# The MLP's second product in half-height matmul pairs: 64 rows of the array for one token tile, 64 for another

## The chip, the cores and the metric

The kernel runs on one core of a Trainium2 chip, in one launch. The metric is the device time of that launch in microseconds, as the median of several runs. The core's engines are TensorE (PE in the profile; its weight loads are listed apart as PEld), VectorE (DVE), ScalarE (ACT), GpSimd (POOL) and SyncE (SP). Each has its own queue of instructions, and the queues wait for one another through semaphores.

## The reference, cut to what matters

One layer of a hybrid transformer block on 1024 tokens of width 1024: a token mixer (a pooling branch and a neighbourhood attention with context keys), a projection, and then the MLP with a squared ReLU. All in float32. The part around the change:

```python
def _sq_relu_mlp(h, w1, w2):
    return jnp.square(jax.nn.relu(h @ w1)) @ w2

    x = x + gt1 * _rmsnorm(mix_x, g_post_mix[l])
    y_x = _sq_relu_mlp(_modulate(x, g_pre_mlp[l], sh2, sc2), w_mlp_in[l], w_mlp_out[l])
    x = x + gt2 * _rmsnorm(y_x, g_post_mlp[l])
```

`h @ w1` is 1024x1024 by 1024x4096, the second product is 1024x4096 by 4096x1024.

## The kernel before, in words

Products in float32 are made of three matmuls in the type fp32r (`three`, lines 197 to 200): each operand is split into a high part and a low part that holds the remainder, and high x high, high x low and low x high are summed in PSUM. In the trace these matmuls are listed as f32, like the plain f32 matmuls of the attention.

Both MLP products are done by a Strassen-like scheme of seven half-size products in place of eight. The hidden layer (4096 wide) is kept in DRAM in seven combinations of its quarters (`hidd`: A11, A12, A22, S1 to S4), each as 8 pages of 128 x 1024: 128 hidden units as rows, two units' blocks of 512 tokens side by side. The second product reads them back. Its seven products are called P1 to P7. Each has 8 groups; a group is one page of hidden values (hi and lo) with one page of weight combinations (hi and lo).

A group (`group`) sums into four PSUM banks, one for each tile of 128 tokens (`ps[0]` to `ps[3]`; the hidden values are the stationary operand, the weights the moving one with 512 columns). For each token tile (`token_sums`) it walks the two blocks j of the page, three matmuls each: 6 matmuls a tile, 24 a group, all with the full 128 rows and 128 columns of the array. The tile's six matmuls go to its bank one after another, then the next tile follows.

The four lists of banks are x, y, v and z. P1 runs alone into x (8 groups). P6 into y and P2 into x take turns, group by group; then P7 into v and P5 into z; then P4 into v and P3 into z for four groups, and two more groups of P3. The last two groups of P3 and the last four of P4 are done at the end, token tile by token tile, with `token_sums` directly, so that the ends of the rows (`finish`, `end`) overlap with the matmuls of later tiles.

Around the groups: `prepare` (called at the start of each group) loads and splits the operands of the item three places ahead: SP issues the DMAs (`hidden`, `columns`), ScalarE makes the high part (`high_part`, line 146), VectorE the low part (`low_part`, line 152) and the weight combinations. The order on PE, ScalarE, VectorE and SP in this part is as written in the code (`in_order`); POOL is left out of that. POOL has little to do here: before the second group of P1 it issues the four DMAs of `mod_gain` (line 243), before the fourth the four DMAs of `mod_out` (line 253), which wait for a product of VectorE (line 247) and that for eight small matmuls (line 236); at the end it makes one reciprocal root per row tile (`rsqrt_of`, line 140).

Elsewhere the kernel has two kinds of matmuls that use only a part of the array: the attention's scores (line 984) contract over 64 rows, for two heads in the two row halves, into two banks; the modulation sums (lines 236 and 401) use 32 of the array's columns, four of them side by side.

Of the kernel before, what the change touches and what calls it, by code (L numbers as in the profile page):

```python
# [18 lines left out]
P = 128  # L19
# [7 lines left out]
HD = 64  # L27
# [53 lines left out]
def hybrid_block(ctx, tc, x, ctx_in, w_mod, b_mod, gp1, gp2, w_in, pool_w, rpb, w_out, w1, w2, vectors,  # L81
                 mask, edge, out):
    nc = tc.nc
# [19 lines left out]
    @contextmanager  # L103
    def in_order(*engines):
        block = nc.cur_bb
        n = len(block.bb.instructions)
        last = {}
        yield last
        assert nc.cur_bb is block
        for i in block.bb.instructions[n:]:  # L110
            if i.engine in engines:
                if i.engine in last:
                    tc.add_manual_dep(i, last[i.engine].name,
                                      mybir.DependencyInfo(mybir.DependencyClass.NoSync, mybir.DependencyReason.DATA),
                                      reason="order")
                last[i.engine] = i
# [80 lines left out]
    def three(ps, ahi, alo, bhi, blo, first, last, more=False):  # L197
        nc.tensor.matmul(ps, ahi, bhi, start=first, stop=False, skip_group_check=more)  # L198
        nc.tensor.matmul(ps, ahi, blo, start=False, stop=False, skip_group_check=more)  # L199
        nc.tensor.matmul(ps, alo, bhi, start=False, stop=last, skip_group_check=more)  # L200
# [70 lines left out]
    with tc.tile_pool(name="ps1", bufs=6, space=PSUM) as ps1, tc.tile_pool(name="tmp1", bufs=3) as tmp:  # L271

        def bank(name):
            if name[:2] == "pm" or name in ("pxt1_0", "pxt0_2", "pxt1_7", "pct2", "pct3"):
                return lasting(name)
            return ps1.tile([P, 512], F32, tag="mm", name=name)
# [7 lines left out]
        last = startup.enter_context(in_order(ET.PE, ET.Activation, ET.DVE, ET.SP, ET.Pool))  # L284
# [276 lines left out]
        for k in range(KT):  # L561
            for i in range(2):
                o = (k % 2) * 256 + i * P
# [178 lines left out]
        with tc.issue_after(last[ET.DVE]), tc.issue_after(last[ET.Activation]):  # L742
            for i in range(2):
                ps = bank(f"pvc{i}")
# [49 lines left out]
        rows = [("sc", 4, k) for k in range(4, KT)] + [("a", 2, k) for k in range(KT)]  # L794
# [35 lines left out]
        for n, m in enumerate((4, 5, 6, 7, 0, 1, 2, 3)):  # L830
            ps = bank(f"pv{m}")
# [99 lines left out]
        with in_order(ET.PE, ET.Pool, ET.Activation, ET.DVE, ET.SP) as pooling:  # L931
            banks = {of: [bank(f"p{of}{j}") for j in range(2)] for of in "KQ"}
            use(-1)
            for step, (n, of, j) in enumerate([(n, of, j) for n, of in products for j in range(2)]):
                half_product(n, of, j, banks[of])
                use(step)
                if step in (5, 9, 17):
                    name = {5: "S1", 9: "S4", 17: "S3"}[step]
# [4 lines left out]
                if step in (7, 11):  # L943
                    name = {7: "S4", 11: "S3"}[step]
# [11 lines left out]
    with (  # L956
# [195 lines left out]
        with in_order(ET.PE, ET.Activation, ET.DVE, ET.SP) as projected:  # L1152
# [7 lines left out]
            for i in range(N + 4):  # L1160
# [12 lines left out]
                if i > 3:  # L1173
                    weighed(i - 4)
                    if i % 8 == 3:
                        j = i // 8 - 1
# [22 lines left out]
                if 8 < i < N and i % 8 == 7:  # L1199
                    j = i // 8 - 1  # L1200
# [9 lines left out]
                else:  # L1210

                    t = i - N
# [51 lines left out]
    with tc.tile_pool(name="ps2", bufs=6, space=PSUM) as ps2:  # L1264
# [6 lines left out]
      with ExitStack() as tmp2:  # L1271
# [28 lines left out]
        rows, root = {}, {}  # L1300
# [233 lines left out]
        NG = NPAIR // 2  # L1534
# [256 lines left out]
        made = {}  # L1791
        coming = list(items)

        def prepare():
            i = coming.pop(0) if coming else None
            if i:
                made[i] = operands(*i, split_pages if i in (("P4", NG - 2), ("P4", NG - 1)) else None)
# [39 lines left out]
        with tc.issue_after(first[ET.PE]), in_order(ET.PE, ET.Activation, ET.DVE, ET.SP):  # L1837
# [12 lines left out]
            def token_sums(ps, t, groups, first, last, more):  # L1850
                n = 2 * len(groups)
                for j in range(n):
                    a, w = groups[j // 2]
                    o = (j % 2) * 512
                    three(ps[t], a[0][:, o + t * P : o + (t + 1) * P], a[1][:, o + t * P : o + (t + 1) * P],
                          w[0][:, o : o + 512], w[1][:, o : o + 512], first and j == 0, last and j == n - 1, more=more)

            def group(ps, name, g, more=False, last=False):
                prepare()
                for t in range(4):  # L1860
                    token_sums(ps, t, [made.pop((name, g)) if t == 3 else made[name, g]], g == 0 and not more,
                               last or g == NG - 1, more)


            sq = [sm(f"sy{h}", NT) for h in range(2)]
            rows = {}
# [33 lines left out]
            for g in range(NG):  # L1900
                if g == 1:
                    gain = mod_gain(gp2, page("gpb")[:, :256], nc.gpsimd)
                if g == 3:
                    mod_gate("b", acc_b[-1], gain, lambda name: pg)
                    mod_out("b", acc_b[-1])
                group(x, "P1", g)
# [4 lines left out]
            for g in range(NG):  # L1911
                group(y, "P6", g)
                if g == NG // 2:
                    G2 = gate_page("b")
                if g == NG - 1:
                    u2 = halves("u2")
                    for t in range(4):
                        nc.vector.tensor_tensor(u2[t], y[t], s1[t], add)
                group(x, "P2", g, more=True)
# [71 lines left out]
```

## Time and profile before

| | |
|---|---|
| time, median of 3 runs | 1032.65 us (1032.61 to 1032.82) |
| span of the profiled execution | 1030.8 us; its own time lies some 1.85 us above, if it was like the median |
| PE busy | 1017.8 us, 5782 matmuls |
| PE weight loads | 834.2 us, 5782 |
| DVE, ACT, POOL busy | 751.8, 543.7, 110.7 us |
| second product, first matmul to last | 718.0 to about 1023 us |
| granted TensorE clock | 0.998 on average |

The span runs from the first to the last instruction of the profiled execution. A matmul's duration in the trace is the time from its issue to its last result; matmuls overlap, so the price of one in a row of many is the distance between two starts, which a count over a stretch of time gives. `x16` behind a row of the order of time means that 16 instructions of a kind were merged; the row's time then runs from the first start to the last end. In a row of a group, `128*128 128x512` is the array's rows and columns in use and then the moving operand.

### The profile page before, as it was taken

The numbers are of one execution on the slowest core, as the hardware profiler recorded it, in microseconds if no ns is written. First come the engines' busy times: TensorE is split into PE (matmuls) and PEld (weight loads), VectorE is DVE, ScalarE is ACT, GpSimd is POOL, SyncE is SP. The second block draws the span as 40 slices with busy tenths as digits, with TensorE's granted clock in tenths as the row PEclk, the third lists the DMA queues.
The fourth block names the chain that finished last, engine by engine and source line by source line (L and its number), as shares of the span: only waits on it lengthen the run. The fifth ranks groups of instructions, "written<-read, shape, count | busy, mean of one in ns | idle before, by whom it ended". The sixth has DMA issues, their size and how long they took to land.

```text
span 1030.8 us, 15588 instructions
## 1 busy us (share of the span) xinstructions
PE 1017.8 (99%) x5782; PEld 834.2 (81%) x5782; DVE 751.8 (73%) x1187; ACT 543.7 (53%) x941; POOL 110.7 (11%) x168
## 2 busy tenths in 40 slices
PE   8999999999999999999999999999999999999997
PEld 6788888877887888888888888888888888888885
DVE  5588767858996587878998887855766666547576
ACT  7573255328887556776655544555543334334431
POOL 3011200244311311310000000000000000000001
PEclk9999999999999999999999999999999999999999
DMA  9999798632337866795786666637967766555556
GB/s 343 332 255 338 246 265 296 204 86 80 72 95 194 203 180 200 253 237 168 267 269 210 204 210 214 205 122 241 327 220 271 248 226 220 202 180 189 176 182 211
DMA packets 123132, 222.68 MB, mean 216 GB/s; under 512 B 9456, under 2 KB 55152, under 8 KB 123056
## 3 DMA queue, kind: packets, MB, share of 16 engines
q1 hardware_dynamic: 96560, 171.14, 50.4%
q0 software_dynamic: 9360, 19.58, 9.5%
q10 hardware_dynamic: 17136, 30.97, 8.0%
q8 instruction: 45, 0.74, 0.3%
q14 instruction: 31, 0.25, 0.1%
HBM read 168.16 MB, written 52.45 MB: 214 GB/s over the span
## 4 chain that ended last, share of the span: by engine, by line
PE 95%; DMA 2%; ACT 1%; DVE 1%; issue 0%; SPq 0%; DVEq 0%; POOLq 0%; ACTq 0%
PE pu L449 4%; PE S L984 4%; PE pa L1060 3%; PE phv L198 3%; PE phz L198 3%; PE phx L198 3%; PE pyx L198 3%; PE phx L200 3%; PE phv L199 3%; PE phx L199 3%; PE pyx L199 3%; PE pyx L200 3%; PE pyv L199 3%; PE pyv L198 3%; PE pyz L199 3%; PE pyz L198 3%
## 5 line engine op out<-in xcount | busy, mean ns | idle before, releaser
L1007 ACT ACTIVATE sp<-sp,nm 128x640 f32<-128x640 f32 (+1 forms) x64 | 51.4, 803 | 20.0 <-DVE nm L998 19.6
L1577 ACT ACTIVATE c<-c 128x512 f32<-128x512 f32 x48 | 30.3, 632 | 47.0 <-DVE c L1697 28.2
L146 ACT CAST wpS<-S 128x512 fp32r<-128x512 f32 x64 | 38.7, 616 | 26.4 <-PE phv L200 9.2
L198 PE MATMUL phx<-thB,wpA 128*128 128x512 f32 x128 | 50.2, 392 | 0.0
L200 PE MATMUL phx<-thB,wpA 128*128 128x512 f32 x128 | 49.8, 389 | 0.0
L199 PE MATMUL phx<-tlB,wpA 128*128 128x512 f32 x128 | 49.8, 389 | 0.0
L152 DVE TENSOR_TENSOR wpS<-S,wpS 128x512 fp32r<-128x512 f32 x64 | 43.4, 685 | 8.3 <-ACT wpS L146 8.3
L998 DVE CUSTOM_DVE_ANT_0 sp<-S,tab 128x640 f32<-128x640 f32 (+1 forms) x56 | 42.9, 803 | 8.8 <-PE S L984 7.3
L1578 ACT ACTIVATE c<-c 128x512 f32<-128x512 f32 x48 | 30.3, 631 | 15.1 <-DVE sa L1660 12.3
L140 POOL TENSOR_TENSOR ry<-vy,nhalf 128x1 f32<-128x1 f32 x8 | 5.9, 740 | 280.7 <-DVE vy L138 280.7
L198 PEld LDWEIGHTS phx<-thB,wpA 128*128 128x128 f32 x128 | 24.0, 188 | 5.5 <-ACT s L1628 0.5
L984 PE MATMUL S<-kT,q 64*128 64x384 f32 (+1 forms) x128 | 27.9, 495 | 0.3 <-DVE nm L998 0.3
L200 PEld LDWEIGHTS phx<-thB,wpA 128*128 128x128 f32 x128 | 24.0, 188 | 5.0
L199 PEld LDWEIGHTS phx<-tlB,wpA 128*128 128x128 f32 x128 | 24.0, 188 | 4.9
L1060 PE MATMUL pa<-pt,v 128*64 128x128 f32 x352 | 25.9, 279 | 0.6 <-ACT px L1040 0.2
L1045 DVE COPY pt<-T 128x512 f32<-128x512 f32 x32 | 22.0, 686 | 5.5 <-PE T L1026 5.5
L198 PE MATMUL phv<-thT,wpA 128*128 128x512 f32 x64 | 25.1, 392 | 0.0
L198 PE MATMUL phz<-thB,wpS 128*128 128x512 f32 x64 | 25.0, 391 | 0.0
L200 PE MATMUL phv<-thT,wpA 128*128 128x512 f32 x64 | 24.9, 389 | 0.0
L199 PE MATMUL phv<-tlT,wpA 128*128 128x512 f32 x64 | 24.9, 389 | 0.0
L200 PE MATMUL phz<-thB,wpS 128*128 128x512 f32 x64 | 24.9, 389 | 0.0
L199 PE MATMUL phz<-tlB,wpS 128*128 128x512 f32 x64 | 24.9, 389 | 0.0
(1100 smaller groups left out, 3359.7 us busy)
## 6 DMA issues: line engine op xcount, KB each, us to landing
b<-in_w SPq DMA_DIRECT2D x64, 512.0 KB, 4.2
hrS<-hdS SPq DMA_DIRECT2D x32, 512.0 KB, 5.1
hrA<-hdA SPq DMA_DIRECT2D x24, 512.0 KB, 5.5
wm<-in_w_mod SPq DMA_DIRECT2D x16, 512.0 KB, 9.7
wa_0w<-in_w SPq DMA_DIRECT2D x16, 512.0 KB, 5.3
wa_1w<-in_w SPq DMA_DIRECT2D x16, 512.0 KB, 4.5
hdA<-c ACTq DMA_DIRECT2D x32, 256.0 KB, 2.8
hdS<-sa ACTq DMA_DIRECT2D x32, 256.0 KB, 2.7
```

The costliest lines, as they stand in the source:

```text
L146: nc.scalar.copy(hi, src)
L152: nc.vector.tensor_tensor(lo, src, hi.bitcast(F32), sub)
L198: nc.tensor.matmul(ps, ahi, bhi, start=first, stop=False, skip_group_check=more)
L199: nc.tensor.matmul(ps, ahi, blo, start=False, stop=False, skip_group_check=more)
L200: nc.tensor.matmul(ps, alo, bhi, start=False, stop=last, skip_group_check=more)
L449: nc.tensor.matmul(pus[b][j], wk(wgt, k, low, j * P, P), r, start=(k == 0 and n == 0), stop=(k == KT - 1 and n == 2))
L984: nc.tensor.matmul(S[e][:, c0 : c0 + keys.shape[1]], q[hs, cols], keys[hs], start=True, stop=True)
L998: nc.vector.tensor_tensor_reduce(out=to, in0=s, in1=bt, scale=1.0, scalar=BIG, op0=add, op1=ALU.min, accum_out=nm)
L1007: nc.scalar.activation(sp, sp, AF.Exp, bias=least[i, e], scale=-1.0, accum_out=sums[i][:, e : e + 1])
L1060: nc.tensor.matmul(pa[e * HD : (e + 1) * HD, cols], v[:, f : f + HD], turns[i][:, e, c] if c < 4 else fifths[i][:, :, (e + 1) * HD : (e + ...
L1577: nc.scalar.activation(r, src, AF.Relu)
L1578: nc.scalar.activation(r, r, AF.Square)
```

## The change

`group` no longer calls `token_sums`. It goes through the group in four quarters with two token tiles each: (0, 1), (2, 3), (1, 0), (3, 2). Within a quarter every former matmul of 128 rows becomes two of 64 rows: the rows 0 to 63 of the operands for the first tile named, the rows 64 to 127 for the second, next to each other in the order of PE, into two different banks. In the third and fourth quarter the tiles change places, so that after all four each bank has had both halves of the contraction. 24 matmuls of 128 rows become 48 of 64 rows, with 512 moving columns as before.

The two halves of the array never write one bank at the same time: the first matmul of a quarter waits for the end of the last matmul of the quarter that used these two banks before. The wait goes over POOL: a `nop` on POOL's queue, after the last matmul of each quarter, and a dependency of the first matmul of the next quarter on the same banks upon that `nop`. There are four such `nop`s in a group, 200 in all. The dictionary `crossings` keeps the last one of each list of banks and pair of tiles, also across groups. The matmuls at the end (`token_sums` on z and v) stay as they were.

```diff
+            crossings = {}
+
+            def after(i, before):
+                tc.add_manual_dep(i.ins, before.ins.name,
+                                  mybir.DependencyInfo(mybir.DependencyClass.Sync, mybir.DependencyReason.DATA),
+                                  reason="rows of the array")
+
             def group(ps, name, g, more=False, last=False):
                 prepare()
-                for t in range(4):
-                    token_sums(ps, t, [made.pop((name, g)) if t == 3 else made[name, g]], g == 0 and not more,
-                               last or g == NG - 1, more)
+                a, w = made.pop((name, g))
+                begin, end = g == 0 and not more, last or g == NG - 1
+                for n, tokens in enumerate(((0, 1), (2, 3), (1, 0), (3, 2))):
+                    crossing = crossings.pop((id(ps), n % 2), None)
+                    for j in range(2):
+                        o = j * 512
+                        for i, (al, wl) in enumerate(((0, 0), (0, 1), (1, 0))):
+                            for rows, t in zip((slice(0, HD), slice(HD, P)), tokens):
+                                mm = nc.tensor.matmul(ps[t], a[al][rows, o + t * P : o + (t + 1) * P], w[wl][rows, o : o + 512],
+                                                      start=begin and n < 2 and j + i == 0,
+                                                      stop=end and n > 1 and j == 1 and i == 2, skip_group_check=True)
+                                if crossing:
+                                    after(mm, crossing)
+                                    crossing = None
+                    crossings[id(ps), n % 2] = nc.gpsimd.nop()
+                    after(crossings[id(ps), n % 2], mm)
```

## The prediction

> **What bounds the kernel now.** First the page's span, busy shares and chain, then one stretch of the second product, then its order of time.
>
> ```profile
> span 1030.8 us, 15588 instructions
> PE 1017.8 (99%) x5782; PEld 834.2 (81%) x5782; DVE 751.8 (73%) x1187; ACT 543.7 (53%) x941; POOL 110.7 (11%) x168
> ...
> PE 95%; DMA 2%; ACT 1%; DVE 1%; issue 0%; SPq 0%; DVEq 0%; POOLq 0%; ACTq 0%
> ```
> ```profile
> 736.00:1016.00 280.00, 280.00 (x1237) 231.85 (x1236) 183.34 (x178) 114.07 (x136) 6.21 (x9) 1.00 0.64 221
> ```
> ```profile
> 800.14 0.39 PE L200 MATMUL pyy<-t_3h,hhS_3l 128*128 128x512 f32 x1
> ...
> 802.86 0.39 PE L200 MATMUL pyx<-b_3h,hhA_3l 128*128 128x512 f32 x1
> ```
> ```profile
> 800.15 0.19 PEld L198 LDWEIGHTS pyx<-b_3h,hhA_3h 128*128 128x128 f32 x1
> ```
>
> TensorE is the bound: 95% of the chain, and busy for all 280.00 us of the stretch from 736 to 1016 us, at a granted clock of 1.00. The 1237 matmuls there come every 280.00/1237 = 226.4 ns (I use 226.5). VectorE is busy for 183 of the 280 us and ScalarE for 114, so nobody else is near. A matmul's 0.39 us is its latency, not its price: they overlap. The load for the next matmul starts 0.01 us after a matmul starts and takes 0.19 us, inside the 0.2265. So the loads are already beside the matmuls, and the question of this change is whether a pair of half-height matmuls goes through in less than, just as much as, or more than 226.5 ns.
>
> **The change part by part.** *The matmuls.* 50 groups of 24 go through the edited function (8 each of P1, P6, P2, P7, P5, 4 of P4, 6 of P3): 1200 full matmuls become 1200 pairs of 64 rows, 2400 instructions, each half with a load of its own. The 144 of the tail stay. No trace row has a 64-row fp32r matmul; the nearest are the attention scores, 64-row f32 pairs on two banks:
>
> ```profile
> 227.05 0.30 PEld L984 LDWEIGHTS S<-kT,q 64*128 64x128 f32 x4 [0.35 <-issue]
> 227.06 0.92 PE L984 MATMUL S<-kT,q 64*128 64x384 f32 x4
> ...
> 227.80 0.60 PE L984 MATMUL S<-kcT,q 64*128 64x256 f32 x4
> 228.24 0.14 PEld L1026 LDWEIGHTS pa<-ident,rb 64*128 64x128 f32 x1 [0.24 <-DVE rb L1013]
> 228.24 0.27 PE L1026 MATMUL pa<-ident,rb 64*128 64x64 f32 x1
> ```
> ```profile
> 66.54 1.91 PE L564 MATMUL pct<-ident,c 128*128 128x128 f32 x16
> 68.20 0.71 PE L449 MATMUL pu<-hx,wu1h 128*128 128x512 f32 x2
> ```
> ```profile
> 734.38 0.64 PE L236 MATMUL pgb<-accb,ones 128*32 128x256 f32 x8
> 734.95 0.50 PE L198 MATMUL pyx<-b_3h,hhA_3h 128*128 128x512 f32 x1
> 735.89 0.42 DVE L247 TENSOR_TENSOR accb<-pgb,gpb 128x256 f32<-128x256 f32 x1
> ```
> ```profile
> L984 PE MATMUL S<-kcT,q x128: 376/376/480, 218.8 to 319.6; 64*128 64x256 f32 x128
> ```
> (An f32 product shows as two matmuls, a transpose as one.) Two pairs of 256 columns take 228.24 - 227.80 = 0.44 us, 0.22 a pair, 0.86 ns a column. Eight of 256 columns in quarters of the array's width (L236) take 0.64 us with the latency of the last, about 0.38 for this width: 0.26 for the first four, so four side by side go at the pace of two. Full-height f32 matmuls exist only as transposes (L564), (68.20 - 66.54)/16 = 0.104 us for 128 columns, 0.81 ns a column. So halves do go through side by side, in about the time of one full matmul of the same width, and not faster than it. Carried over to fp32r: a pair costs what the full matmul costs, 226.5 ns, and 1200 pairs change the sum by 0. The added loads are covered too: four take 0.30 us, side by side, under the running pair.
>
> Could the pair shed something? By its pace an f32 matmul of 256 columns occupies the array about as long as an fp32r one of 512. Durations, beside the 376 of L984:
>
> ```profile
> L198 PE MATMUL pyx<-b_0h,hhA_0h 128*128 128x512 f32 x16 | 6.2, 389 | 0.0
> ```
> ```profile
> L690 PE MATMUL pkc<-hc,wk0h x8: 387/395/398, 76.5 to 85.3; 128*128 128x512 f32 x8
> ...
> L690 PE MATMUL pkc<-hc,wk0l x8: 277/280/281, 76.7 to 85.5; 128*128 128x256 f32 x8
> ```
> An fp32r matmul of 512 is 13 ns longer than the f32 half of 256: 389 against 376. With the same latency past the stream, 389 - 226.5 = 163, the streams are 226 and 213. If that is a price of exchanging weights in the whole array, halves may hide it: up to -13 x 1200 = -15.6 us. If it is a price of streaming 4-byte columns, they can't. The fp32r rows of 512 and 256 columns (387/395 and 277/280) differ by 110 to 115 ns; 13 ns per matmul whatever its width would leave 213/2 = 107 between them, 13 ns spread over 512 columns gives 113. Nearest is the second, so I take 0 and keep -15.6 as the lower end. The upper end for the stream is no concurrency at all, +226.5 x 1200 = +272 us.
>
> [...]
>
> *Change of array shape.* Rows where 64-row pairs follow and precede full matmuls:
>
> ```profile
> 218.51 0.39 PE L200 MATMUL pqv<-S3h,wQT3l 128*128 128x512 f32 x1
> 218.83 0.70 PE L984 MATMUL S<-kcT,q 64*128 64x256 f32 x4
> 219.36 0.60 PE L984 MATMUL S<-kT,q 64*128 64x256 f32 x4
> 219.89 0.50 PE L198 MATMUL pqv<-hx,wQT4h 128*128 128x512 f32 x1
> 220.23 0.40 PE L199 MATMUL pqv<-hx,wQT4h 128*128 128x512 f32 x1
> ```
> Into the pairs: 0.32 instead of 0.2265, and 0.53 instead of 0.44: +0.18. Out: 0.53 instead of 0.44, then 0.34 instead of 0.2265: +0.20. The new kernel goes in at P1 and out at the tail, +0.4 us; the gate's column-tiled matmuls in the middle already pay for such a change today.
>
> *The crossings.* 200 nops on POOL's queue, each behind the last matmul of a quarter group; 192 matmuls wait for one (the first two of each of the four lists of sums have none). Within a group, and between groups of one product that follow each other, six pairs of the other quarter lie between, 6 x 226.5 = 1.36 us, of which 0.39 goes until the last matmul has ended: 0.97 us of cover for PE to POOL to PE. No row shows that trip; its parts:
>
> ```profile
> 228.43 0.82 DVE L998 CUSTOM_DVE_ANT_0 sp<-S,tab 128x640 f32<-128x640 f32 x1 [0.25 <-PE S L984]
> 229.18 0.08 DVE L998 DVE_READ_ACCUMULATOR2_ANT nm<- 128x1 f32 x1
> 229.32 1.33 PE L984 MATMUL S<-kT,q 64*128 64x384 f32 x3 [0.30 <-DVE nm L998]
> ```
> ```profile
> 707.32 1.99 POOL L243 DMA_DIRECT2D gpb<-in_gp  x4 [111.49 <-PE phz L200]
> 736.59 1.93 POOL L253 DMA_DIRECT2D gb<-accb  x4 [27.28 <-DVE accb L247]
> ...
> 1019.25 0.55 POOL L140 TENSOR_TENSOR ry<-vy,nhalf 128x1 f32<-128x1 f32 x1 [2.62 <-DVE vy L138]
> ```
> From PE to a waiting engine 0.03 (228.43 after 227.80 + 0.60), to POOL up to 0.28 (736.59 after 735.89 + 0.42); the nop between 0 and POOL's 0.55 for its smallest tensor operation; back to PE 0.06 (229.32 after 229.26). Sum 0.09 to 0.89 us: inside 0.97 at both ends, so I cost the steady crossings at 0; with the cover gone each microsecond of lateness costs some 120 us (100 crossings within groups and 18 between groups have only this cover, the others a whole group of the other product).
>
> POOL's own DMAs stand in the same queue. Those of L243 are now behind the nops of P1's first group, at about 723.8 instead of 707.32, busy to 725.8; they must have landed by 734.4. The second group's first nop slips to 725.8, and is wanted at 726.2: 0 to 0.5, I take 0.1. Those of L253 end at 736.59 + 1.93 = 738.52; the nop behind them lets go a matmul that is due at 734.95 + 0.3 + 12 x 0.2265 = 737.97: +0.6 to +1.2, I take 0.7. After that POOL has nothing until the tail.
>
> *The end of each product.* Two token tiles now end with the third quarter of the last group and two with the fourth, instead of one per quarter. Their readers are four copies or sums of about 0.7 us; the sums are written again a whole group (5.4 us) later, so 0.
>
> Sum: 0 + 0.4 + 0.1 + 0.7 = +1.2 us on the span of 1030.8, 1032.0. The median of the runs, 1032.65, lies 1.85 above the profiled span; with the same 1.85 the time is 1033.9, +0.12%. That is less than the 0.2% (2.1 us) which a measurement of this kernel tells from no change.
>
> **The rivals.** *A, forecast: pairs at the old pace, crossings covered.* 1033.9; own range 1031.5 to 1037.5 (a fee of 3 ns a pair more would be +3.6).
>
> *B, the halves shed the 13 ns.* 1033.9 - 15.6 = 1018.3 in full; at the 0.22 us of the f32 pair, -6.5 x 1200 = -7.8, 1026.1. The 13 ns over the f32 row speak for it, the 256-column fp32r rows and the equal price of f32 pairs and f32 full matmuls against it.
>
> *C, the crossing takes the place of what was gained or more: the trip over POOL is longer than its cover.* It decides from 0.97 + 2.1/120 = 0.99 us on; a trip of 1.2 us costs 0.23 x 120 = 28, 1061. For it: the upper bound of the parts, 0.89, is near, and a pair that runs faster shortens the cover. Against it: the lower sum is 0.09.
>
> *D, fp32r halves don't run side by side*, because two full-rate 4-byte streams or two full-rate writes into PSUM don't fit, which f32 pairs at half the column rate never asked for: +272 us, 1306. For it: no row shows such a pair; against it only the f32 pairs. [...]
>
> **How the numbers follow.** A 0.42, B 0.28, C 0.20, D 0.10. A's range lies across +0.2%, so it gives 0.24 to no change and 0.18 to slower; B is faster; C and D are slower: 0.28, 0.24, 0.48. The predicted time is A's. The range takes in B and C, 1018 to 1062, and leaves out D and the far ends of C.
>
> **What would show it.** In the changed trace, two 64-row matmuls some 0.01 us apart on two banks and the next two 0.2265 us after: A; 0.213 to 0.22: B; 0.45: D. Waits of PE on POOL at the first matmul of the third and fourth quarter: C; one alone near 738 us is the step of L253. The gpb transfers move behind 723 us. The forecast falls if any price repeats 1200 or 120 times that the f32 rows don't have.

## The result, and the profile after

| | before | changed |
|---|---|---|
| time, median of 20 runs | 1032.73 us | 1034.77 us |
| ratio | | 1.0017, 95% interval 1.001 to 1.0023 |
| span of the profiled execution | 1030.8 us | 1033.3 us |

The change costs 0.17% by the ratio; the two medians differ by 2.0 us (0.20%). 1033.9 was predicted (+0.12%). The profiled execution of the changed kernel is the longest of its twenty runs (1035.77 us; the median of their spans is 1032.6), so single places in it can cost more than they do in a typical run. The page of the changed kernel, and a stretch of 250 us of the second product of both kernels (first the changed one), with the busy time and count of each engine:

```profile
span 1033.3 us, 18193 instructions
PE 1019.2 (99%) x6982; PEld 834.6 (81%) x6982; DVE 751.9 (73%) x1187; ACT 543.5 (53%) x941; POOL 110.9 (11%) x168
...
PE 93%; DMA 3%; ACT 1%; DVE 1%; issue 1%; SPq 0%; POOL 0%; DVEq 0%; POOLq 0%; ACTq 0%
```
```profile
741.00:991.00 250.00, 250.00 (x2210) 206.83 (x2208) 156.97 (x143) 101.49 (x116) 0.00 (x0) 1.00 0.65 217
```
```profile
741.00:991.00 250.00, 250.00 (x1105) 207.01 (x1104) 156.88 (x143) 101.52 (x117) 0.00 (x0) 1.00 0.63 217
```

1200 more matmuls and loads, and in the same 250 us exactly twice as many halves as full matmuls: 2210 against 1105. A pair takes 250/1105 = 226.2 ns, as a full matmul did. (The count takes in matmuls that lie across the ends of the stretch; from start to start it is 226.7 ns on average in both kernels.) In order of time the two halves of a pair stand merged as x2, one pair every 0.226 us:

```profile
800.04 0.39 PE L1875 MATMUL pyy<-t_3h,hhS_3l 64*128 64x512 f32 x2
800.27 0.39 PE L1875 MATMUL pyy<-t_3h,hhS_3h 64*128 64x512 f32 x2
800.50 0.39 PE L1875 MATMUL pyy<-t_3l,hhS_3h 64*128 64x512 f32 x2
```

What was lost stands in three places. At the start of P1 and at the tail, where the array changes its shape:

```profile
717.90 0.39 PE L200 MATMUL phv<-thT,wpA 128*128 128x512 f32 x1
718.22 0.50 PE L1875 MATMUL pyx<-b_0h,hhA_0h 64*128 64x512 f32 x2
718.56 0.40 PE L1875 MATMUL pyx<-b_0l,hhA_0h 64*128 64x512 f32 x2
```
```profile
992.48 0.39 PE L1875 MATMUL pyz<-b_5h,hhS_5l 64*128 64x512 f32 x2
992.80 0.50 PE L198 MATMUL pyz<-b_6h,hhS_6h 128*128 128x512 f32 x1
993.14 0.40 PE L199 MATMUL pyz<-b_6l,hhS_6h 128*128 128x512 f32 x1
```

Each time 0.32 and 0.34 instead of twice 0.2265: 0.2 us in, 0.2 us out. And near 738 us, in the group before which POOL issues the DMAs of the gate:

```profile
737.99 0.39 PE L1875 MATMUL pyx<-b_3h,hhA_3l 64*128 64x512 f32 x2
739.62 0.50 PE L1875 MATMUL pyx<-b_3h,hhA_3h 64*128 64x512 f32 x2 [1.24 <-POOLq L1881]
739.95 0.39 PE L1875 MATMUL pyx<-b_3l,hhA_3h 64*128 64x512 f32 x2
```
```profile
728.79 1.98 POOL L243 DMA_DIRECT2D gpb<-in_gp  x4 [132.68 <-PE pyx L1875]
738.29 1.93 POOL L253 DMA_DIRECT2D gb<-accb  x4 [7.53 <-DVE accb L247]
```
```profile
737.58 0.42 DVE L247 TENSOR_TENSOR accb<-pgb,gpb 128x256 f32<-128x256 f32 x1 [1.96 <-DMA gpb<-in_gp]
```

The pair due at 738.22 starts at 739.62, and the next comes 0.33 later: 1.4 + 0.1 us. It waits for a nop (L1881) that stands on POOL's queue behind three of the four DMAs of L253. These are late because the product of L247 was held for 1.96 us by the transfer of L243, and that one was issued at 728.79 and not at 707.32. Together 0.4 + 1.5 = 1.9 us of the 2.5 between the profiled spans; the rest lies outside of the second product's groups.

### The profile page after: what moved, and what is told of

Same layout as the page of the kernel before. It is cut to its first block, busy times and chain, and to the rows that moved or that the text cites. A ratio compares the mean times of both kernels' runs of the same rounds, so it can differ in the third digit from the quotient of the medians.

```text
span 1033.3 us, 18193 instructions
## 1 busy us (share of the span) xinstructions
PE 1019.2 (99%) x6982; PEld 834.6 (81%) x6982; DVE 751.9 (73%) x1187; ACT 543.5 (53%) x941; POOL 110.9 (11%) x168
## 4 chain that ended last, share of the span: by engine, by line
PE 93%; DMA 3%; ACT 1%; DVE 1%; issue 1%; SPq 0%; POOL 0%; DVEq 0%; POOLq 0%; ACTq 0%
PE pyx L1875 8%; PE pyz L1875 7%; PE pyv L1875 6%; PE pu L449 4%; PE pyy L1875 4%; PE S L984 4%; PE pa L1060 3%; PE phz L198 3%; PE phv L198 3%; PE phx L198 3%; PE phx L199 3%; PE phv L199 3%; PE phz L199 3%; PE phx L200 3%; PE phv L200 3%; PE phz L200 3%
## 5 line engine op out<-in xcount | busy, mean ns | idle before, releaser
L198 PE MATMUL phz<-thB,wpS 128*128 128x512 f32 x64 | 25.0, 391 | 0.0
L199 PE MATMUL phy<-tlT,wpS 128*128 128x512 f32 x64 | 24.9, 389 | 0.0
```

## The experiments

Theory N: the pair costs what the full matmul costs, crossings are covered, the loss is the stall near 738 us and the array's shape. Its rival Z: the pairs do gain, and the 192 waits give it back. Four kernels beside the kernel before (1032.99 us there).

**The changed kernel again.**

> The changed kernel once more, beside the variants. Theory N (a pair costs what the full matmul costs; the loss is one stall of POOL's queue, 1.5 us with the refill, and 0.4 us of array shape changes): 1.9 us above the kernel before. Theory Z (the pairs gain several ns each and the 192 waits give it back): the same number here, so this run only anchors the others.

1035.01 us, ratio 1.0016 (1.0007 to 1.0025): the same as the first time. Its profiled execution, though, has the stall nearly closed, 738.53 to 738.81 in place of 0.2265, 0.06 us. The product of L247 was held for only 0.88 us there:

```profile
738.30 0.39 PE L1875 MATMUL pyx<-b_3h,hhA_3l 64*128 64x512 f32 x2
738.53 0.45 PE L1875 MATMUL pyx<-b_3h,hhA_3h 64*128 64x512 f32 x2
738.81 0.39 PE L1875 MATMUL pyx<-b_3l,hhA_3h 64*128 64x512 f32 x2
```
```profile
737.15 1.93 POOL L253 DMA_DIRECT2D gb<-accb  x4 [6.07 <-DVE accb L247]
```

**Pairs without crossings.**

```diff
-                for n, tokens in enumerate(((0, 1), (2, 3), (1, 0), (3, 2))):
+                for n, tokens in enumerate(((0, 1), (2, 3), (0, 1), (2, 3))):
...
-                    crossings[id(ps), n % 2] = nc.gpsimd.nop()
-                    after(crossings[id(ps), n % 2], mm)
```

> Pairs that never change places: quarters three and four use the same row halves for the same tiles as quarters one and two, so that no wait and no nop is needed. It leaves out part of the sums (half of the contraction is summed twice, the other half not at all); the number and size of matmuls and loads is that of the changed kernel. Theory N: the stall near 738 us is gone, pairs stay at 226.7 ns, 0.4 to 0.6 us above before. Theory Z: with the waits gone the gain of the pairs shows, more than 2 us below before (5 ns a pair would be 6 us).

1033.23 us, ratio 1.0005 (0.9996 to 1.0013), +0.24 us. No gain comes out when the waits are gone, and the pairs keep their pace (2210 halves in 250 us, as in the changed kernel): Z falls.

```profile
741.00:991.00 250.00, 250.00 (x2210) 206.62 (x2208) 157.65 (x143) 101.51 (x117) 0.00 (x0) 1.00 0.64 219
```

**Crossings without pairs.**

```diff
...
                 for t in range(4):
+                    crossing = crossings.pop((id(ps), t % 2), None)
...
+                            mm = nc.tensor.matmul(ps[t], a[al][:, o + t * P : o + (t + 1) * P], w[wl][:, o : o + 512],
+                                                  start=begin and j + i == 0, stop=end and j == 1 and i == 2,
+                                                  skip_group_check=True)
+                            if crossing:
+                                after(mm, crossing)
+                                crossing = None
+                    crossings[id(ps), t % 2] = nc.gpsimd.nop()
+                    after(crossings[id(ps), t % 2], mm)
```

> The other part alone: full 128-row matmuls as before, with the nops and waits of the change (a nop after each token tile's six matmuls, and the first matmul of the tile after the next waits for it). Theory N: matmuls at 226.7 ns, one stall at POOL's DMAs of 1 to 2 us, no change of the array's shape: 1.0 to 2.0 us above before. Theory Z: the waits cost several us with no gain against them, 5 us or more above before.

1033.19 us, ratio 1.0002 (0.9993 to 1.0011), +0.2 us: the waits cost nothing, which speaks against Z once more. The stall that N expected here did not come. The place of POOL's DMAs between the nops is the scheduler's: here L243 is issued at 733.34, later than in the changed kernel, and L253 only after 745 us, where nobody waited for it in the profiled execution.

```profile
733.34 1.98 POOL L243 DMA_DIRECT2D gpb<-in_gp  x4 [136.68 <-PE pyx L1874]
```

**The changed kernel with the gate's DMAs on ScalarE's queue.**

```diff
-                    gain = mod_gain(gp2, page("gpb")[:, :256], nc.gpsimd)
+                    gain = mod_gain(gp2, page("gpb")[:, :256], nc.scalar)
...
-                    mod_out("b", acc_b[-1])
+                    mod_out("b", acc_b[-1], nc.scalar)
```

> The changed kernel with the eight DMAs of mod_gain and mod_out issued from ScalarE's queue instead of POOL's, so that no nop stands behind a DMA. Theory N: the stall of 1.5 us is gone, 0.4 to 0.6 us above before, and no wait of PE on POOL. If instead late crossings elsewhere make up the loss, it stays at about 2 us above before.

1033.85 us, ratio 1.0007 (0.9998 to 1.0016), +0.86 us, and no wait of PE on POOL is left in the second product's part of the profile. Of the changed kernel's 2.0 us in this comparison 1.2 went with the DMAs' place. Some 0.3 us more than N's 0.4 to 0.6 remain; they lie outside the span, whose median over the runs is 1031.7 us against 1031.2 before (+0.5, as N said) and 1032.8 in the changed kernel.

**The second product alone.** The times above also hold what varies ahead of and behind the second product. One profiled execution of each kernel, from the start of P1's first matmul to the start of the last matmul, separates the parts:

| | first matmul of P1 | last matmul | between |
|---|---|---|---|
| before | 717.97 | 1023.18 | 305.21 us |
| crossings without pairs | 718.86 | 1024.07 | 305.21 us |
| pairs without crossings | 719.16 | 1024.78 | 305.62 us |
| changed, the gate's DMAs on ScalarE's queue | 718.31 | 1023.92 | 305.61 us |
| changed, second profile | 718.53 | 1024.25 | 305.72 us |
| changed, first profile | 718.22 | 1025.37 | 307.15 us |

The crossings add nothing, the pairs add the 0.4 us of the array's shape, and only the place of POOL's DMAs adds to that, 0.1 us in one execution and 1.5 in the other.

**Both halves of a pair in the same rows.**

```diff
-                            for rows, t in zip((slice(0, HD), slice(HD, P)), tokens):
+                            for rows, t in zip((slice(0, HD), slice(0, HD)), tokens):
```

> Both matmuls of a pair on rows 0 to 63, the other half of the array idle; it leaves out the upper half of the contraction. Theory S (the halves run side by side, which alone keeps the pair at 226.7 ns): now one after the other, 453 ns a pair, 1200 x 226.7 = 272 us more, about 1306 us. Rival (64-row matmuls of fp32r are cheaper by themselves, their pace being set by the issue): well under 1300 us.

1305.63 us (one run): +272.4 us above before, as S said. One matmul of 64 rows takes as long as one of 128 (two every 0.45 us), and only the other half of the array makes the pair free:

```profile
800.45 0.61 PE L1875 MATMUL pyx<-b_7h,hhA_7l 64*128 64x512 f32 x2
800.90 0.61 PE L1875 MATMUL pyx<-b_7h,hhA_7h 64*128 64x512 f32 x2
```

**How long may a crossing take.** The nop replaced by one memset, and by two:

```diff
+            spare_page = tmp.tile([P, 512], F32, tag="spare", name="spare", bufs=1)
...
-                    crossings[id(ps), n % 2] = nc.gpsimd.nop()
+                    crossings[id(ps), n % 2] = nc.gpsimd.memset(spare_page, 0.0)
```

> Each nop replaced by one memset of 128x512 on POOL (about 0.5 us by the 0.96 us of the 128x1024 ones), so the trip PE to POOL to PE is 0.6 to 0.75 us instead of about 0.12. Theory N with a cover of 0.97 us: same as the changed kernel within 1 us, apart from the stall near 738 us. Rival (the cover is used up already): 118 waits x 0.5 us, some 60 us more.

> Each nop replaced by two such memsets, trip 1.1 to 1.3 us, past the cover of 0.97 us. Theory N: 118 waits x 0.15 to 0.35 us, 18 to 41 us above the changed kernel, and PE waits on POOL in the third and fourth quarter of every group. If the cover is longer than reckoned: no more than cross_1.

1045.27 us, ratio 1.0123 (1.0108 to 1.0138), and 1060.35 us, ratio 1.0268 (1.025 to 1.0285). The first is 10 us more than expected, but not by the crossings. The very first memset starts only at 729.70, where the changed kernel had its first nop at 719.9. The author's reading is that the new tile takes over memory and that POOL waits for what still used it: the profile names a low part of VectorE (`b_3l`) as what ended the wait here, and a DMA of an earlier tile (`hdS`) in the two-memset kernel, whose first memset starts at 728.6. PE stands for 8.5 us, and goes on at a granted clock of 0.50 for ten pairs, 0.43 us apart:

```profile
721.39 0.39 PE L1876 MATMUL pyx<-b_0h,hhA_0l 64*128 64x512 f32 x2
730.28 0.80 PE L1876 MATMUL pyx<-b_0h,hhA_0h 64*128 64x512 f32 x2 [8.49 <-POOL spare L1882]
730.87 0.63 PE L1876 MATMUL pyx<-b_0l,hhA_0h 64*128 64x512 f32 x2
731.30 0.63 PE L1876 MATMUL pyx<-b_0h,hhA_0l 64*128 64x512 f32 x2
...
735.12 0.39 PE L1876 MATMUL pyx<-b_0h,hhA_0l 64*128 64x512 f32 x2
```

Behind that the two differ cleanly. 225 us of each, first with one memset, then with two:

```profile
775.00:1000.00 225.00, 225.00 (x1988) 185.91 (x1986) 140.99 (x129) 93.21 (x107) 87.28 (x166) 1.00 0.63 212
```
```profile
775.00:1000.00 225.00, 225.00 (x1902) 173.14 (x1900) 132.91 (x121) 87.66 (x101) 166.87 (x318) 1.00 0.62 205
```
```profile
769.95 1.12 POOL L1883 MEMSET spare<- 128x512 f32 x2 [0.27 <-PE pyx L1876]
...
771.01 0.39 PE L1876 MATMUL pyx<-b_6h,hhA_6l 64*128 64x512 f32 x2
...
771.53 1.11 POOL L1883 MEMSET spare<- 128x512 f32 x2 [0.46 <-PE pyx L1876]
...
772.40 0.39 PE L1876 MATMUL pyx<-b_6h,hhA_6l 64*128 64x512 f32 x2
772.70 0.50 PE L1876 MATMUL pyx<-b_7h,hhA_7h 64*128 64x512 f32 x2
773.04 0.40 PE L1876 MATMUL pyx<-b_7l,hhA_7h 64*128 64x512 f32 x2
```

With one memset a pair takes 225/994 = 226.4 ns: 0.53 us of memset in the trip is covered. With two a pair takes 225/951 = 236.6 ns on average. There the last matmul of a quarter ends at 771.01 + 0.39 = 771.40. The pair that waits for it would be due at 772.40 + 0.23 = 772.63, so the cover is some 1.2 us. It starts at 772.70, right after the memsets from 771.53 end at 772.64: a trip of 1.30 us. It is 0.07 late, and the next one 0.11, as behind the stall at 739.62. With one memset less the trip is some 0.7 us. The cover thus ends between trips of 0.7 and 1.3 us. Of the 25 us between the two-memset kernel and the changed one (1060.35 against 1035.01), 10 are the first wait, as in the one-memset kernel. Of the other 15, a little under the 18 to 41 expected, late starts at crossings make up some 11 in the profiled execution; part of the rest is two more waits of PE on POOL, near 737 and 752 us.

**What the 13 ns are.** Three kernels without pairs. First half of the stationary columns:

```diff
+                m = P if begin else HD
...
+                            nc.tensor.matmul(ps[t][:m], a[al][:, o + t * P : o + t * P + m], w[wl][:, o : o + 512],
...
```

> What the 13 ns of an fp32r matmul over the f32 half are: the kernel before with only 64 of the 128 stationary columns (64 tokens of each tile) in 1104 of the 1200 matmuls of the groups; it leaves out the other tokens' sums. Weight loads are half as long, the stream of 512 columns is the same. Theory C (13 ns belong to streaming 4-byte columns): 226.7 ns stays, same as before within 1 us. Theory W (they belong to loading or exchanging 128 weights): 220 ns, some 7 us less.

1036.98 us, ratio 1.0035 (1.0022 to 1.0049): neither theory. A matmul takes 250/1090 = 229 ns there:

```profile
741.00:991.00 250.00, 250.00 (x1090) 149.80 (x1089) 154.32 (x140) 101.41 (x116) 0.00 (x0) 1.00 0.62 215
```

The loads are shorter, though not half as long (149.8 us busy for 1089, 137.6 ns each, against 207.0 for 1104, 187.5 ns); the matmuls are not. Why they got longer was not found. Then half of the moving columns:

```diff
+                            for c in (0, 256):
+                                o = j * 512
+                                nc.tensor.matmul(ps[t][:, c : c + 256], a[al][:, o + t * P : o + (t + 1) * P],
+                                                 w[wl][:, o + c : o + c + 256], start=begin and j + i == 0,
...
```

> The kernel before with every matmul of the groups split into two of 256 moving columns, 2400 full-height fp32r matmuls, each with its own load. Theory C: twice 113 ns, same as before within 3 us, if a load fits under 113 ns. Theory W (13 ns per matmul whatever its width): 120 ns each, 1200 x 13 = 16 us more. A load that takes longer than 113 ns to follow another gives more than that and leaves it open.

It changes part of the sums. 1049.56 us, ratio 1.0163 (1.0143 to 1.0183), +16.8 us, close to the 16 of W: two every 0.24 us.

```profile
800.26 0.40 PE L1867 MATMUL pyy<-t_3h,hhS_3h 128*128 128x256 f32 x2
800.50 0.40 PE L1867 MATMUL pyy<-t_3l,hhS_3h 128*128 128x256 f32 x2
```
```profile
741.00:991.00 250.00, 250.00 (x2086) 250.00 (x2085) 146.93 (x133) 95.56 (x109) 0.00 (x0) 1.00 0.61 208
```

```profile
L1867 PE MATMUL pyx<-b_4h,hhA_4h 128*128 128x256 f32 x32 | 6.4, 283 | 0.0
```

250/2086 = 119.8 ns for 256 columns and 226.2 for 512 lie on a line of 106.4 ns for 256 columns plus 13.4 for each matmul. Two points always lie on a line, and the loads are busy all the time here, so that a load that can't follow another within 120 ns isn't excluded. Last, operands of 2 bytes:

```diff
+        def split_two(raw, hi, lo):
+            nc.scalar.copy(hi, raw)
+            nc.vector.tensor_tensor(lo, raw, hi, sub)
+            return hi, lo
+
         def split_pages(name, raw):
-            hi, lo = page(f"{name}h", F32R), page(f"{name}l", F32R)
-            split(raw, hi, lo)
-            return hi, lo
+            return split_two(raw, *(page(f"{name}{n}").bitcast(BF16)[:, :1024] for n in "hl"))
...
-            made = made or high_low
+            made = made or high_low_two
```

> What the 13 ns of an fp32r matmul are, once more: the kernel before (full height, no crossings) with the second product's high and low parts written in bfloat16 instead of fp32r, so that both operands of its 1344 matmuls have 2 bytes. Shapes, loads and counts are the same; the sums lose the accuracy of the third part of the mantissa. Theory C (the 13 ns belong to streaming columns of 4 bytes): 213 to 216 ns a matmul, 1344 x 11 to 13.3 = 15 to 18 us below before. Theory W (they belong to exchanging weights, whatever their size): 226.7 ns stays, same as before.

1018.05 us, ratio 0.9859 (0.9842 to 0.9875): 14.7 us under before.

```profile
741.00:980.00 239.00, 239.00 (x1109) 108.33 (x1107) 157.22 (x144) 102.18 (x117) 0.00 (x0) 1.00 0.66 226
```

239/1109 = 215.5 ns a matmul, some 11 ns under the fp32r matmul; 1344 x (226.2 - 215.5) = 14.4 us. The loads shrink as well (108 us busy for 1107, against 207 for 1104), so this run alone can't say whether the 11 ns belong to the bytes of the load or to those of the stream. Taken with the 256-column run it looks like a cost per matmul. This kernel is faster than both, but it isn't the same computation: each operand of the second product is two bfloat16 parts instead of two fp32r parts.

## Why the prediction was right

*The pairs at the old pace* held to a nanosecond (226.2 against 226.2), and with it the term 0 for 1200 pairs, which the forecast rests on. That halves run side by side, and that this is what pays for them, was carried over from f32 pairs; the kernel with both halves in the same rows shows it for fp32r (+272.4 us, the +272 of case D).

*"13 ns spread over 512 columns ... Nearest is the second"* is the step that failed, though the term it led to stands. The 110 to 115 ns between the fp32r rows of 512 and 256 columns were durations, in a stretch where the two widths alternate. In streams of one width the durations are 389 and 283 ns, 106 apart, and the distances from start to start 226.2 and 119.8, 106 apart as well, which speaks for a price of 13 ns per matmul (not shown for certain, because of the loads in the 256-column run). By the prediction's own alternative the halves might then have hidden it. They didn't: each pair still takes what the full matmul took, the 13 ns included. So "halves may hide it" did not come true either, and that this part of the working ended at 0 is luck. What exactly the 13 ns pay for stays open; the run with half the stationary columns didn't fit either reading.

Loads for one half under matmuls of the other half brought nothing: 2210 halves against 1105 full ones in 250 us, with the loads busy for 206.83 and 207.01 us of it.

*Change of array shape*, +0.4: 0.2 in and 0.2 out, as reckoned.

*The crossings*, 0: shown three ways, by the crossings without pairs (+0.2 us, interval through 1; 305.21 us of second product in both profiles), by the pairs without crossings, and by the memsets. The cover of 0.97 us was reckoned one pair too short. With six pairs between, the waiting pair starts seven distances after the last matmul of the earlier quarter starts: 7 x 0.2265 - 0.39 = 1.20 us, as the two-memset kernel shows (771.40 to 772.63). Rival C would have needed a trip above that, and its 28 us for a trip of 1.2 us would have been about 0. For a nop it makes no difference. The trip itself was at the low end of 0.09 to 0.89 us: at 738 us PE starts some 0.06 us after the nop that it waited for. The rows of POOL's DMAs (0.28) and of its small tensor operation (0.55), the upper bounds, have nothing to do with a nop, whose entry in the trace lasts 17 ns.

*POOL's DMAs in the same queue*, +0.1 and +0.7: the place was right, near 738 us, but not the size (1.5 us in the first profile) and not the way that the loss came about. The step that was off is "behind the nops of P1's first group, at about 723.8". POOL's order isn't written out, and the DMAs of L243 came 5 us later, at 728.79, behind nops of the second group. Their landing then was late for VectorE (1.96 us), which the prediction had excluded. How late depends on the execution: the slowest of the four transfers landed 7.1 us after its issue in the first profile and 5.6 in the second, and PE lost 1.5 and 0.06 us. The 0.7 for L253 by itself is not there. In the second profile its DMAs start 1.48 us after the group's first matmul (737.15 and 735.67), no later than in the kernel before (736.59 and 734.95, 1.64), the nop stands behind three of the four, and PE loses 0.06 us; in the first profile they start 2.93 us after it (738.29 and 735.36). So the loss came by the term priced at 0.1. With these DMAs on another queue the runs lost 1.2 us less; that the sum of both terms, 0.8, lies near this is partly luck.

*A at 0.42, C at 0.20, D at 0.10, B at 0.28*: A it was, with +0.17%, just under the 0.2% that the prediction took as the limit between no change and slower, in the range that it gave to A.

## What to carry to other kernels

In this kernel a pair of 64-row matmuls took 226.2 ns on the two row halves and some 0.45 us in the same rows (+272.4 us for 1200 pairs): where a product has only 64 rows to contract, try the halves side by side. The full contraction cut in two gained nothing, since one full matmul took the same 226.2 ns. Before giving a cross-engine wait to a queue that looks idle, see what else is in that queue and who fixes its order: in the first profile the wait on POOL was free 191 times out of 192, and the one behind a DMA that itself waits for an engine cost 1.5 us, more than everything else (0.4 us of the array's shape). Where matmuls of 4-byte operands bound a kernel, look at the type and the width first; in this kernel 512 columns cost 226 ns in fp32r, two times 256 cost 240, and 512 in bfloat16 cost 215.5.

## What the runs showed of the hardware

After an idle time of 8.5 us (the one-memset kernel, above) TensorE went on at half pace: pairs 0.43 us apart from 730.87 to 734.71, then 0.23. The granted clock, before the last two columns of a row, is 0.50 while the pairs are slow. It fell between 724 and 725 us (0.92 on average there), some 3 us after the last matmul had ended at 721.78; the old distance is back at 735.12, 4.8 us after TensorE went on:

```profile
724.00:725.00 1.00, 0.00 (x0) 0.00 (x0) 0.00 (x0) 1.00 (x2) 0.00 (x0) 0.92 0.92 293
730.28:734.71 4.43, 4.43 (x20) 3.50 (x22) 0.51 (x1) 0.00 (x0) 1.86 (x4) 0.50 0.97 347
```

The stall of 1.2 us near 738 us in the changed kernel brought no such thing: behind it came one distance of 0.33 and then 0.23, at a granted clock of 1.00 (737 to 742 us). Beyond these times the runs don't show what moves the clock.
